# Two of four later modulation sections summed in the output-merge stage, and the residual-gate rows spread by a transpose and a repeating DRAM load

## The chip, the cores and the metric

One core of one Trainium2 chip runs the whole program. The time is device microseconds of one execution. The engines named below are TensorE (PE, with its weight loads as PEld), VectorE (DVE), ScalarE (ACT), GpSimd (POOL) and SyncE (SP). SP, ACT and POOL also issue the transfers between DRAM and on-chip memory; each of them issues its own in program order, among its other work.

## The reference, cut to what matters

The program is one layer of a streaming encoder on 1024 tokens of width 1024, all in float32.

```
mod = silu(c) @ ada_w + ada_b                       # 6 sections of 1024 numbers each
sh1, sc1, g1, sh2, sc2, g2 = split(mod, 6)
h = rmsnorm(x, ln1_g) * (1 + sc1) + sh1
q, k, v, cb, cc, cx, ga, gb = split(h @ w_in)
y_a = stick_breaking_attention(rmsnorm(q), rmsnorm(k), v)
y_b = cb * causal_dwconv3(cc * cx)
merged = sigmoid(ga) * (y_a @ w_branch_a) + sigmoid(gb) * (y_b @ w_branch_b)
x = x + g1 * (merged @ w_out)
h = rmsnorm(x, ln2_g) * (1 + sc2) + sh2
x = x + g2 * ((silu(h @ w_ffn_gate) * (h @ w_ffn_up)) @ w_ffn_down)
```

What matters here is `mod`. Sections 0 and 1 (sh1, sc1) are needed at once and are summed at the start. Sections 2 to 5 are the "later" ones: 2 is g1, the residual gate of the output projection; 3 and 4 are sh2 and sc2, which enter the second normalisation; 5 is g2, the residual gate of the last product. g1 and g2 multiply along the width, which lies in the columns of the tiles there, so they have to stand as a row that is the same on all 128 partitions.

## The kernel before, in words

A float32 product is made of three matmuls: each factor is split into a rounded high part (a copy on ACT, `whi`, `hi`) and a low rest (a subtraction on DVE, `wlo`, `lo`), and high times high, high times low and low times high are added in PSUM. So each weight tile costs ACT one pass and DVE one pass, and each finished PSUM bank costs a pass on DVE or ACT. PE is kept busy by all of this arriving in time; the 128x512 matmul is the unit nearly everywhere.

The stages in order, with their place in the profiled execution: the start (sections 0 and 1 of `mod`, v and k) to about 200 us; q, the convolution and the gates ("gate stage", to about 597 us); attention with the B branch's products as filler (to about 993 us); the product with `w_branch_a` and the merge ("merge stage", to about 1086 us); the output projection and second normalisation; the SwiGLU products; the down projection.

**Gate stage.** The loop over `gates` runs 20 products, each cut Strassen-like into seven block products `p1..p7`; the last eight are the sigmoid gates (sections named 4 and 3 there, four each). The sums of weight blocks (`ws`) are made on POOL, their splits on ACT and DVE, and the results `c` are combined on DVE straight from PSUM (`tt(nc.vector, c.., p.., c.., ...)`, all on line L136). Between them the loop pulls the generator `mods_later`, five steps after each gate of the last eight (`next(ml, None)`).

**mods_later.** For a section, `ada_w` is seen as 8 tiles of 128 x 1024 (`ada_2[q, k]`, 512 KB each): the 128 partitions are 128 outputs, the 1024 columns the inputs. `silu(c)` stands in `cab` on all partitions. One DVE instruction per tile (`tensor_tensor_reduce`, shown on the profile as CUSTOM_DVE_ANT_0 on L640, followed by a short read of its accumulator) multiplies and adds along the columns, and leaves 128 outputs as one column of `msum`. I call it a "section sum". Four sections make 32 of them. The tiles are loaded on ACT's queue into buffers that the gate stage has anyway (`uu`, `sq`, `tr`). For sections 3 and 4 the 8 columns plus bias go to `mod`. For 2 and 5 the columns are spread to a row on all partitions by 8 matmuls each against the identity `dm` (the loop body that line L653 stands for; the profile counts 32 of 128x128 for the two sections, as a float32 matmul is recorded more than once), copied by ACT to `uu`, and written as 512 KB to `d_g[e]` in DRAM. They are loaded back as 512 KB where they are used: `g1b` on ACT's queue at the head of the output projection, `g2b` on SP's queue in the down projection.

**Merge stage.** Sixteen products (m, n) of 24 matmuls each into PSUM banks of the tag `pj`, of which there are two. After each, DVE multiplies the bank by the gate (`sgi`, L1148), adds the stored B branch (`mb`, L1149), ACT takes the high part (L1153) and DVE the rest (L1154). A bank can be written again when its L1148 is done. The weights of the next stage (`w_o`) are loaded and split ahead here by `preload_wo`, at the product (6, 0) in program order. POOL has no work in this stage.

**What sets the order.** The instruction order on each engine is fixed at build time by a list scheduler that works from its own estimates; the engines then run their lists strictly in order. A wait at the head of an engine's list so holds up all that is behind it. Buffers are taken in turn, and a stage's buffers reuse the memory of the stage before it, so a load into a new buffer waits for the last reader or writer of what lay there.

Of the kernel before, what the change touches and what calls it, by code (L numbers as in the profile page):

```python
# [17 lines left out]
P = 128  # L18
T = 1024
D = 1024  # L20
# [10 lines left out]
def block_kernel(tc, x, x_t, cols, ada_1, ada_2, ada_row, w_q, w_kv, w_cg, w_a, w_b, w_o, w_g, w_u, w_d, out):  # L31
# [43 lines left out]
    d_y = drp.tile([KT, P, T], F32, name="d_y")  # L75
    d_mb = drp.tile([KT, P, T], F32, name="d_mb")
    d_b = drp.tile([1, 512], F32, name="d_b")
    d_g = [drp.tile([P, D], F32, name=f"d_g{e}") for e in range(2)]
    d_x1 = drp.tile([KT, P, D], F32, name="d_x1")

    d_t = {q: drp.tile([P, 2, 4, 512], F32, name=f"d_t{q}") for q in (6, 3, 5, 4)}
# [540 lines left out]
    def g_big():  # L622
        return gp.tile([P, T + 2], F32, tag="uu", bufs=2, name=nm("uu"))

    def mods_later():

        csb, cab = g_big()[:, :D], gp.tile([P, D], F32, tag="tr", bufs=2, name=nm("cab"))
        nad = 0
        nc.scalar.dma_start(cab, ada_row[0:1, :].broadcast_to([P, D]))
        nc.scalar.activation(csb, cab, AF.Sigmoid)  # L630
        tt(nc.vector, cab, cab, csb, ALU.mult)
        yield
        for q, sec in enumerate(SECS):
            ms = gp.tile([P, 8], F32, tag="msum", bufs=2, name=nm("msum"))
            for k in range(KT):
                tag = ("uu", "sq", "uu", "sq", "tr")[nad % 5]
                ad = g_big()[:, :D] if tag == "uu" else gp.tile([P, D], F32, tag=tag, bufs=2, name=nm("ad"))
                nad += 1
                nc.scalar.dma_start(ad, ada_2[q, k])
                nc.vector.tensor_tensor_reduce(out=ad, in0=ad, in1=cab, scale=1.0, scalar=0.0, op0=ALU.mult,  # L640
                                               op1=ALU.add, accum_out=ms[:, k:k + 1])
                yield
            if sec in (3, 4):
                tt(nc.vector, mod[:, sec - 1], ms, acol[:, sec - 1], ALU.add)
                continue
            e = 0 if sec == 2 else 1
            tt(nc.vector, ms, ms, gcol[:, e], ALU.add)
            yield
            gb_ = g_big()[:, :D]
            for n in range(2):  # L650
                ps = g_ss()
                for i in range(4):
                    nc.tensor.matmul(ps[:, i * P:(i + 1) * P], ms[:, 4 * n + i:4 * n + i + 1].broadcast_to([P, P]), ident,  # L653
                                     start=True, stop=True)
                nc.scalar.activation(gb_[:, n * 512:(n + 1) * 512], ps, AF.Copy)
            nc.scalar.dma_start(d_g[e], gb_)
            yield

    def g_ss():
        return ps_tr()  # L660
# [69 lines left out]
    for g, (sec, j) in enumerate(gates):  # L730
        raw, raw2 = raws
        p1, p2 = pre[g] if g in pre else (g_prod(g_split(raw[:, :512]), 0), g_prod(g_split(raw[:, 512:]), 1))
        a11, a12, a21, a22 = raw[:, :512], raw[:, 512:], raw2[:, :512], raw2[:, 512:]
        s1, s2_, s3, s4 = (gp2.tile([P, 512], F32, tag=f"ws{q}", bufs=1, name=nm("ws")) for q in range(4))
        with tc.high_priority() if g == 0 else ExitStack():
            tt(nc.gpsimd, s3, a11, a21, ALU.subtract)
            tt(nc.gpsimd, s2_, a22, s3, ALU.subtract)
            w6 = g_split(s2_)
        tt(nc.gpsimd, s1, a21, a22, ALU.add)
        ws4 = nc.gpsimd.tensor_tensor(out=s4, in0=a12, in1=s2_, op=ALU.subtract)  # L740
# [48 lines left out]
        tt(nc.vector, c21, p4, c21, ALU.add)  # L789
        later()  # L790
        put(c21, j + 4, 0)
        if g + 1 == len(gates):
            for _ in eq:
                pass
        for _ in range((5 if sec in (3, 4) else 0) if g + 1 < len(gates) else 50):
            next(ml, None)
    sg2.close()
    sg_.close()
# [300 lines left out]
    fqpool.close()  # L1099


    swx = ExitStack()
    wx = swx.enter_context(tc.tile_pool(name="wpx", bufs=1, side="right", reuse_waits="tile"))
    w_pre = []

    def preload_wo():

        for j in range(3):
            raw = wx.tile([P, 1024], F32, tag="raw", bufs=1, name=nm("raw"))
            nk = 1 if j == 2 else 2  # L1110
# [24 lines left out]
    wa = {}  # L1135
    for m, n in [(0, 0), (1, 0), (0, 1), (1, 1)] + [(m, n) for m in range(2, KT) for n in range(2)]:
        if (m, n) == (KT - 2, 0):
            with tc.issue_after(last_m.ins):
                preload_wo()
        if n == 0:  # L1140
# [11 lines left out]
            mlo[n] = big()  # L1152
        nc.scalar.activation(mh[n][:, m, :], sa, AF.Copy)  # L1153
        nc.vector.tensor_tensor(out=mlo[n][:, m, :], in0=sa, in1=mh[n][:, m, :].bitcast(F32), op=ALU.subtract)  # L1154
    s3.close()
    fpool.close()
    gws.close()
# [27 lines left out]

    los = []
    g1b = dp.tile([P, D], F32, name="g1b")
    nc.scalar.dma_start(g1b, d_g[0])
# [379 lines left out]
    for t in range(4):  # L1568
        nc.scalar.activation(u2t[t], pa[t], AF.Copy)
    with tc.issue_after(last_f[0].ins):  # L1570
        nc.sync.dma_start(g2b, d_g[1])
    pb = [bank() for t in range(4)]
    down(pb, 1, lambda j: R1[j][:, c0])
    for t in range(4):
# [118 lines left out]
```

## Time and profile before

| what | value |
|---|---|
| runs, median (lowest to highest) | 1822.8 us (1822.58 to 1824.99), 3 runs |
| profiled execution, first to last instruction | 1822.9 us |
| granted TensorE clock, mean | 0.995 |
| PE busy / PEld busy | 1794.7 us (98%) / 1492.0 us (82%) |
| DVE / ACT / POOL busy | 1362.9 us (75%) / 809.6 us (44%) / 367.4 us (20%) |
| moved by DMA | 359.57 MB, mean 197 GB/s |
| section sums of `mods_later` (L640) | 32, from 444.1 to 541.2 us |
| spreading matmuls (L653) | 32, in two groups, at 493.9 and 594.9 us |

A matmul row of the trace starts about every 0.227 us in a full run of 128x512 matmuls, though each is shown as 0.39 us long, since they overlap. What PE loses is therefore read from the distance between starts, not from its busy time. The bracket at the end of a timeline row gives idle time in front of the instruction and what ended it.

### The profile page before, as it was taken

Reading aid. Unit: us, or ns where it says so; the run is one execution under the profiler, and the core shown is the slowest. Engines: PE = TensorE matmul, PEld = TensorE weight load, DVE = VectorE, ACT = ScalarE, POOL = GpSimd, SP = SyncE. Lnnn points to the kernel's source line nnn. Section 1 sums busy time; section 2 is a strip of 40 time slices with the busy share of each in tenths; the row PEclk is TensorE's granted clock in tenths of the full one; section 3 lists DMA queues with packets and bytes.
Section 4 is the critical chain, followed back from the end, with each engine's and each line's share of the span. In section 5 each row is a group of like instructions: output and inputs, shape, how many; then the busy total and the mean of one; then the engine's idle time right before and its main releaser. Section 6 shows DMA issues by size and latency. Waiting matters only on the chain.

```text
span 1822.9 us, 24550 instructions
## 1 busy us (share of the span) xinstructions
PE 1794.7 (98%) x8629; PEld 1492.0 (82%) x8629; DVE 1362.9 (75%) x1980; ACT 809.6 (44%) x1510; POOL 367.4 (20%) x277
## 2 busy tenths in 40 slices
PE   8999999999999899999999999999999999999999
PEld 6888877888778788888888888877888888878887
DVE  5876586778894699999997554699877878644776
ACT  5534363333433466666675221764444344322321
POOL 0024234632232000000000000115434444200000
PEclk9999999999999999999999999999999999999999
DMA  9479644223684977696654546424443444299876
GB/s 381 162 247 386 235 163 141 81 98 125 230 287 155 265 203 185 191 336 172 160 135 153 184 155 204 129 91 183 164 150 139 150 169 155 107 347 346 274 230 220
DMA packets 165102, 359.57 MB, mean 197 GB/s; under 512 B 15522, under 2 KB 60906, under 8 KB 163828
## 3 DMA queue, kind: packets, MB, share of 16 engines
q1 hardware_dynamic: 128300, 289.65, 48.6%
q10 hardware_dynamic: 35672, 64.68, 9.9%
q0 software_dynamic: 1008, 3.67, 0.5%
q8 instruction: 69, 1.13, 0.3%
q14 instruction: 53, 0.43, 0.1%
HBM read 247.32 MB, written 110.66 MB: 196 GB/s over the span
## 4 chain that ended last, share of the span: by engine, by line
PE 83%; DVE 8%; DMA 5%; issue 2%; ACT 1%; POOL 0%; SPq 0%; ACTq 0%; DVEq 0%; POOLq 0%
PE e L131 7%; PE e L133 7%; PE e L132 7%; PE pj L293 7%; PE pj L131 5%; PE pj L133 5%; PE pj L132 5%; PE pj L995 4%; PE pj L997 4%; PE pj L996 4%; PE e L1521 4%; PE e L1523 4%; PE e L1522 4%; PE tr L919 3%; PE o L935 2%
## 5 line engine op out<-in xcount | busy, mean ns | idle before, releaser
L905 DVE TENSOR_TENSOR_SCAN pt<-pt,mk 128x128 f32<-128x128 f32 (+7 forms) x128 | 172.6, 1348 | 3.2 <-ACT pt L897 3.2
L131 PE MATMUL e<-big,whi 128*128 128x512 f32 x352 | 138.2, 393 | 3.8 <-ACT c L1421 3.8
L132 PE MATMUL e<-big,whi 128*128 128x512 f32 x352 | 137.9, 392 | 0.0
L133 PE MATMUL e<-big,wlo 128*128 128x512 f32 x352 | 137.8, 392 | 0.0
L293 PE MATMUL pj<-whi,big 128*128 128x512 f32 x448 | 133.7, 396 | 3.1 <-ACT big L262 3.1
L136 DVE TENSOR_TENSOR c<-e,c 128x512 f32<-128x512 f32 x138 | 92.9, 687 | 54.8 <-PE e L133 53.8
L131 PE MATMUL pj<-big,whi 128*128 128x512 f32 x320 | 125.3, 392 | 1.6 <-DVE c L136 1.6
L133 PE MATMUL pj<-big,wlo 128*128 128x512 f32 x320 | 124.9, 390 | 0.0
L132 PE MATMUL pj<-big,whi 128*128 128x512 f32 x320 | 124.6, 389 | 0.0
L122 POOL TENSOR_SCALAR rs_m<-ss 128x1 f32<-128x1 f32 x8 | 1.7, 218 | 607.5 <-ACT xn L1324 607.5
L1521 PE MATMUL e<-whi,f 128*128 128x512 f32 (+1 forms) x319 | 121.8, 382 | 0.9 <-ACT whi L1182 0.6
L1522 PE MATMUL e<-wlo,f 128*128 128x512 f32 (+1 forms) x319 | 121.8, 382 | 0.0
L1523 PE MATMUL e<-whi,f 128*128 128x512 f32 (+1 forms) x319 | 121.6, 382 | 0.0
L136 DVE TENSOR_TENSOR c<-pj,c 128x512 f32<-128x512 f32 x140 | 93.1, 682 | 36.0 <-PE pj L133 35.2
L897 ACT ACTIVATE pt<-z,rq 128x512 f32<-128x512 f32 (+1 forms) x192 | 105.1, 576 | 25.4 <-PE z L896 25.0
L995 PE MATMUL pj<-big,whi 128*128 128x512 f32 x256 | 113.9, 445 | 0.0
L136 POOL TENSOR_TENSOR ws<-raw,raw 128x512 f32<-128x512 f32 x40 | 54.1, 1354 | 278.3 <-DMA raw<-w_cg 130.0
L923 DVE TENSOR_TENSOR atl<-tr,ath 128x512 fp32r<-128x512 f32 (+1 forms) x192 | 103.1, 550 | 9.2 <-ACT ath L922 7.2
L922 ACT ACTIVATE ath<-tr 128x512 fp32r<-128x512 f32 (+1 forms) x192 | 93.2, 488 | 33.1 <-PE tr L919 32.2
L132 PE MATMUL e<-rl,whi 128*128 128x512 f32 x264 | 102.8, 390 | 1.5 <-DVE rl L136 1.5
L133 PE MATMUL e<-rh,wlo 128*128 128x512 f32 x264 | 102.7, 389 | 0.0
L131 PE MATMUL e<-rh,whi 128*128 128x512 f32 x264 | 102.7, 389 | 0.0
(269 smaller groups left out, 4863.2 us busy)
## 6 DMA issues: line engine op xcount, KB each, us to landing
f<-d_f SPq DMA_DIRECT2D x77, 512.0 KB, 4.3
d_f<-fs SPq DMA_DIRECT2D x70, 512.0 KB, 3.2
raw<-w_cg SPq DMA_DIRECT2D x40, 512.0 KB, 3.2
raw<-w_u SPq DMA_DIRECT2D x26, 512.0 KB, 3.3
raw<-w_g SPq DMA_DIRECT2D x25, 512.0 KB, 3.6
raw<-w_kv SPq DMA_DIRECT2D x20, 512.0 KB, 4.0
ad<-ada ACTq DMA_DIRECT2D x19, 512.0 KB, 4.5
ld<-ada SPq DMA_DIRECT2D x16, 512.0 KB, 4.3
```

Of the source, the lines that this page charges most:

```text
L131: nc.tensor.matmul(ps, wh[:, k, :], fh[:, k, :], start=(k == 0), stop=False)
L132: nc.tensor.matmul(ps, wh[:, k, :], fl[:, k, :], start=False, stop=False)
L133: nc.tensor.matmul(ps, wl[:, k, :], fh[:, k, :], start=False, stop=(k == 3))
L136: eng.tensor_tensor(out=out, in0=a, in1=b, op=op)
L293: nc.tensor.matmul(ps, a, b, start=(k == 0 and q == 0), stop=(k == KT - 1 and q == 2))
L897: nc.scalar.activation(pt[:, off + s0:off + s0 + m], z[:, :m], AF.Sigmoid, scale=rq[:, 1, i, h:h + 1])
L905: nc.vector.tensor_tensor_scan(out=pt[:, rev], data0=pt[:, rev], data1=mk[:, rev], initial=1.0, op0=ALU.mult, op1=ALU.max)
L923: nc.vector.tensor_tensor(out=tl[:, :nb, c0:c0 + P], in0=src, in1=th[:, :nb, c0:c0 + P].bitcast(F32), op=ALU.subtract)
L995: nc.tensor.matmul(ps, wh, rh_, start=(k == 0), stop=False)
L1521: nc.tensor.matmul(o, sh, w[0][:, c], start=(j == 0), stop=False)
L1522: nc.tensor.matmul(o, sh, w[1][:, c], start=False, stop=False)
L1523: nc.tensor.matmul(o, sl, w[0][:, c], start=False, stop=(j == NJ - 1))
```

## The change

Of the four later sections, 2 and 4 (g1 and sc2) stay in the gate stage, on the same buffers and ACT's queue, with three generator steps per gate in place of five. Sections 3 and 5 (sh2 and g2) are summed by a second generator `mods_last`, pulled one or two steps after each product of the merge stage and drained before (6, 0). It has a pool of its own: `cab3` for silu(c), loaded again from DRAM and turned by one Silu on ACT, three buffers `ad` for the tiles, and `msum`, `mrow`. Its 18 transfers are issued on POOL's queue. The pool lies where attention's score tiles `pt` lay, and the pool of `preload_wo` is now opened after it is closed.

The two gate rows are no longer spread by matmuls. `msum` is 128 wide and cleared by a POOL memset, transposed by one matmul against the identity, its 8 used rows are copied by ACT and written as 4 KB to `d_g[e]`, which is now one row. `g1b` and `g2b` read that row 128 times (`broadcast_to`).

```
-    d_g = [drp.tile([P, D], F32, name=f"d_g{e}") for e in range(2)]
+    d_g = [drp.tile([1, D], F32, name=f"d_g{e}") for e in range(2)]
...
+    def mod_sums(secs, big_, small, cab, queue, bank_):
+
+        nad = 0
+        for sec in secs:
+            q = SECS.index(sec)
+            ms = small([P, P], "msum")
+            if sec in (2, 5):
+                nc.gpsimd.memset(ms, 0.0)
+            for k in range(KT):
+                ad = big_(nad)
+                nad += 1
+                queue.dma_start(ad, ada_2[q, k])
+                nc.vector.tensor_tensor_reduce(out=ad, in0=ad, in1=cab, scale=1.0, scalar=0.0, op0=ALU.mult,
+                                               op1=ALU.add, accum_out=ms[:, k:k + 1])
+                yield
+            if sec in (3, 4):
+                tt(nc.vector, mod[:, sec - 1], ms[:, :KT], acol[:, sec - 1], ALU.add)
+                continue
+            e = 0 if sec == 2 else 1
+            tt(nc.vector, ms[:, :KT], ms[:, :KT], gcol[:, e], ALU.add)
+            yield
+            ps, row = bank_(), small([P, P], "mrow")
+            nc.tensor.transpose(ps[:, :P], ms, ident)
+            nc.scalar.activation(row[:KT], ps[:KT, :P], AF.Copy)
+            queue.dma_start(d_g[e].rearrange("o (k p) -> (o k) p", p=P), row[:KT])
+            yield
...
-            gb_ = g_big()[:, :D]
-            for n in range(2):
-                ps = g_ss()
-                for i in range(4):
-                    nc.tensor.matmul(ps[:, i * P:(i + 1) * P], ms[:, 4 * n + i:4 * n + i + 1].broadcast_to([P, P]), ident,
-                                     start=True, stop=True)
-                nc.scalar.activation(gb_[:, n * 512:(n + 1) * 512], ps, AF.Copy)
-            nc.scalar.dma_start(d_g[e], gb_)
...
+        yield from mod_sums((2, 4), big_, lambda s, t_: g_tile()[:, :P], cab, nc.scalar, g_ss)
...
-        for _ in range((5 if sec in (3, 4) else 0) if g + 1 < len(gates) else 50):
+        for _ in range((3 if sec in (3, 4) else 0) if g + 1 < len(gates) else 50):
             next(ml, None)
...
+    def mods_last():
+
+        cab = mlp.tile([P, D], F32, name="cab3")
+        with tc.issue_after(lastav[0].ins):
+            nc.gpsimd.dma_start(cab, ada_row[0:1, :].broadcast_to([P, D]))
+            nc.scalar.activation(cab, cab, AF.Silu)
+        yield
+        yield from mod_sums((3, 5), lambda i: mlp.tile([P, D], F32, tag="ad", bufs=3, name=nm("ad")),
+                            lambda s, t_: mlp.tile(s, F32, tag=t_, bufs=1, name=nm(t_)), cab, nc.gpsimd,
+                            lambda: pps.tile([P, 512], F32, tag="tr", bufs=NTR, name=nm("tr")))
...
         if (m, n) == (KT - 2, 0):
+            for _ in ml:
+                pass
+            sml.close()
             with tc.issue_after(last_m.ins):
                 preload_wo()
...
+        for _ in range(1 + m % 2):
+            next(ml, None)
...
-    nc.scalar.dma_start(g1b, d_g[0])
+    nc.scalar.dma_start(g1b, d_g[0][0:1, :].broadcast_to([P, D]))
...
-        nc.sync.dma_start(g2b, d_g[1])
+        nc.sync.dma_start(g2b, d_g[1][0:1, :].broadcast_to([P, D]))
```

The lists of the engines after the change, at three places. Line numbers of the change are a few higher than those before it: the section sum is L640 before and L637 in the change, the gate product on DVE L1148 and L1173, the last filler product's L1044 and L1051.

**DVE where the section sums begin (about 450 us).** Here `c_...<-pj_...` combines a finished PSUM bank, `wlo` splits a weight, and each section sum is two rows (the sum and its read-out). Before:

```order
L723 SCALAR_TENSOR_TENSOR gt_3818<-uu_2776,cst,gt_3818 128x512
L136 TENSOR_TENSOR c_3874<-pj_3878,c_3873 128x512
L136 TENSOR_TENSOR wlo_4010<-raw_3869,whi_4009 128x512
L640 ISA uu_3980,msum_3979<-uu_3980,cab_3975 128x1024
L640 ISA msum_3979 128x1
L136 TENSOR_TENSOR wlo_4033<-ws_4027,whi_4032 128x512
L640 ISA ad_4149,msum_3979<-ad_4149,cab_3975 128x1024
L640 ISA msum_3979 128x1
L136 TENSOR_TENSOR wlo_4083<-ws_4028,whi_4082 128x512
L136 TENSOR_TENSOR c_3873<-pj_3844,c_3873 128x512
```

In the change:

```order
L730 SCALAR_TENSOR_TENSOR gt_3818<-uu_2776,cst,gt_3818 128x512
L136 TENSOR_TENSOR c_3874<-pj_3878,c_3873 128x512
L136 TENSOR_TENSOR wlo_4005<-raw_3869,whi_4004 128x512
L136 TENSOR_TENSOR c_3873<-pj_3844,c_3873 128x512
L637 ISA ad_3984,gt_3979<-ad_3984,cab_3975 128x1024
L637 ISA gt_3979 128x1
L637 ISA ad_4141,gt_3979<-ad_4141,cab_3975 128x1024
L637 ISA gt_3979 128x1
```

Before, three section sums stand ahead of the first of these rows and two more among them, so `c_3873`, which empties the bank `pj_3844`, comes behind five; in the change it comes ahead of all of them.

**DVE where they end before (about 540 us).** Before:

```order
L136 TENSOR_TENSOR wlo_4741<-ws_4702,whi_4740 128x512
L640 ISA uu_4996,msum_4826<-uu_4996,cab_3975 128x1024
L640 ISA msum_4826 128x1
L136 TENSOR_TENSOR wlo_4709<-ws_4703,whi_4708 128x512
L136 TENSOR_TENSOR c_4554<-pj_4617,c_4554 128x512
```

In the change:

```order
L136 TENSOR_TENSOR wlo_4701<-ws_4662,whi_4700 128x512
L1217 SCALAR_TENSOR_TENSOR a_10721<-mod,cst 128x8
L136 TENSOR_TENSOR wlo_4669<-ws_4663,whi_4668 128x512
L136 TENSOR_TENSOR wlo_4719<-ws_4664,whi_4718 128x512
L136 TENSOR_TENSOR c_4520<-pj_4583,c_4520 128x512
```

Before, the last section sum stands between the two `wlo` splits that the next block products need (`wlo_4741` and `wlo_4709`); in the change none stands between `wlo_4701` and `wlo_4669`, which answer to them, and six rows lie between the stage's last sum and `wlo_4701`.

**DVE at the head of the merge stage (about 999 us).** `oy` is attention's last output, `mb_...<-pj_...` the emptying of the last filler product's bank, `ya` splits attention's output, `sgi_...<-pj_...` empties the first merge product. Before:

```order
L941 TENSOR_TENSOR oy_9966<-o_9948,otmp_9965 64x256
L136 TENSOR_TENSOR wlo_10122<-raw_10119,whi_10121 128x512
L136 TENSOR_TENSOR ya_10061<-yr_10059,ya_10061 128x512
L136 TENSOR_TENSOR ya_10066<-yr_10064,ya_10066 128x512
L1044 TENSOR_TENSOR mb_9986<-pj_9938,sgi_9936 128x512
L136 TENSOR_TENSOR wlo_10126<-raw_10119,whi_10125 128x512
L136 TENSOR_TENSOR ya_10071<-yr_10069,ya_10071 128x512
L1148 TENSOR_TENSOR sgi_10084<-pj_10088,sgi_10084 128x512
```

In the change:

```order
L637 ISA ad_10092,msum_10091<-ad_10092,cab_10045 128x1024
L637 ISA msum_10091 128x1
L136 TENSOR_TENSOR wlo_10051<-raw_10048,whi_10050 128x512
L637 ISA ad_10095,msum_10091<-ad_10095,cab_10045 128x1024
L637 ISA msum_10091 128x1
L1051 TENSOR_TENSOR mb_9912<-pj_9864,sgi_9862 128x512
L136 TENSOR_TENSOR wlo_10055<-raw_10048,whi_10054 128x512
L637 ISA ad_10133,msum_10091<-ad_10133,cab_10045 128x1024
L637 ISA msum_10091 128x1
L136 TENSOR_TENSOR ya_9987<-yr_9985,ya_9987 128x512
L136 TENSOR_TENSOR ya_9992<-yr_9990,ya_9992 128x512
L1173 TENSOR_TENSOR sgi_10010<-pj_10014,sgi_10010 128x512
```

Two section sums now stand ahead of the emptying of the last filler bank and a third ahead of the first merge product's; the two `ya` splits have moved behind them. The other thirteen follow among the next seven products' rows: the sixteenth stands in front of the emptying of the eighth product's bank.

More of the change, by code (lines that the diff above doesn't have):

```diff
@@ L623, in g_big @@
         return gp.tile([P, T + 2], F32, tag="uu", bufs=2, name=nm("uu"))
+    def mod_sums(secs, big_, small, cab, queue, bank_):
[23 more added lines that the diff above has]
+            yield
     def mods_later():
         csb, cab = g_big()[:, :D], gp.tile([P, D], F32, tag="tr", bufs=2, name=nm("cab"))
-        nad = 0
         nc.scalar.dma_start(cab, ada_row[0:1, :].broadcast_to([P, D]))
@@ L632, in mods_later, with big_ @@
         yield
[L633 to L648, printed above, removed]
-            gb_ = g_big()[:, :D]
-            for n in range(2):
-                ps = g_ss()
-                for i in range(4):
-                    nc.tensor.matmul(ps[:, i * P:(i + 1) * P], ms[:, 4 * n + i:4 * n + i + 1].broadcast_to([P, P]), ident,
-                                     start=True, stop=True)
-                nc.scalar.activation(gb_[:, n * 512:(n + 1) * 512], ps, AF.Copy)
-            nc.scalar.dma_start(d_g[e], gb_)
-            yield
+        def big_(i):
+            tag = ("uu", "sq", "uu", "sq", "tr")[i % 5]
+            return g_big()[:, :D] if tag == "uu" else gp.tile([P, D], F32, tag=tag, bufs=2, name=nm("ad"))
+        yield from mod_sums((2, 4), big_, lambda s, t_: g_tile()[:, :P], cab, nc.scalar, g_ss)
     def g_ss():
@@ L1099, in block_kernel @@
     fqpool.close()
+    sml = ExitStack()
+    mlp = sml.enter_context(tc.tile_pool(name="mlp", bufs=1, side="right", reuse_waits="tile"))
+    def mods_last():
[7 more added lines that the diff above has]
+                            lambda: pps.tile([P, 512], F32, tag="tr", bufs=NTR, name=nm("tr")))
+    ml = mods_last()
     swx = ExitStack()
-    wx = swx.enter_context(tc.tile_pool(name="wpx", bufs=1, side="right", reuse_waits="tile"))
     w_pre = []
     def preload_wo():
+        wx = swx.enter_context(tc.tile_pool(name="wpx", bufs=1, side="right", reuse_waits="tile"))
         for j in range(3):
```

## The prediction

> **What bounds the kernel now.** I read the busy times first, then who PE waited for, then the stretches in which those waits lie, then the distances between matmul starts there.
>
> ```profile
> PE 1794.7 (98%) x8629; PEld 1492.0 (82%) x8629; DVE 1362.9 (75%) x1980; ACT 809.6 (44%) x1510; POOL 367.4 (20%) x277
> ...
> PE e L131 <- ACT c L1421: 3.8, 1, 3.8
> ...
> PE pj L133 <- DVE wlo L136: 2.0, 1, 2.0
> ...
> PE pj L131 <- DVE c L136: 1.6, 3, 0.7
> ...
> PE z L895 <- DMA skh<-d_k: 1.3, 1, 1.3
> ...
> PE pj L995 <- DVE mb L1044: 1.2, 1, 1.2
> ...
> PE z L896 <- DMA skl<-d_k: 0.8, 1, 0.8
> ```
>
> PE sets the end: all its waits (us in total, times, longest) are a few microseconds of 1823. So two things can gain: matmuls that go away, and these few waits. Those on `wlo` and `c` lie in the gate stage, those on `skh` and `skl` at the head of attention, that on `mb` at the head of the merge stage, that on `c` L1421 in the SwiGLU stage. The stretches (us; busy time and instructions of PE, PEld, DVE, ACT, POOL; granted clock; DMA share; GB/s):
>
> ```profile
> 440.00:480.00 40.00, 38.41 (x167) 30.86 (x166) 39.17 (x55) 13.31 (x23) 14.98 (x8) 1.00 0.74 268
> 505.00:541.00 36.00, 34.97 (x154) 28.45 (x152) 35.19 (x54) 11.80 (x20) 11.32 (x7) 1.00 0.81 279
> 1004.00:1042.00 38.00, 37.96 (x167) 31.45 (x168) 19.76 (x30) 9.47 (x15) 0.00 (x0) 1.00 0.57 189
> ```
>
> In the two stretches where the gate stage makes its section sums DVE is full (39.2 of 40, 35.2 of 36 us), and PE's three and one waits come there. In the first half of the merge stage DVE is free nearly half the time and POOL wholly.
>
> **The change part by part.** The profiled span is 1822.9 us against a median of 1822.8, so the sum is made on 1822.9 with nothing around it.
>
> *Matmuls.* The spreading groups go.
>
> ```profile
> L653 PE MATMUL tr<-dm,msum x32: 271/275/275, 493.9 to 596.6; 128*128 128x128 f32 x32
> ...
> 493.92 1.95 PE L653 MATMUL tr<-dm,msum 128*128 128x128 f32 x16
> ...
> 495.62 0.48 PE L131 MATMUL pj<-big,whi 128*128 128x512 f32 x1
> ```
>
> A group holds PE for 495.62 - 493.92 = 1.70 us, two 3.4 us. Two transposes come in; in the group one record is 1.70/16 = 0.11 us, two records each and the slower hand-over around them make some 0.15 us apiece. Net -3.1 us; both lie on PE's chain.
>
> *Waits of the gate stage.* Sixteen sums leave it.
>
> ```profile
> 455.87 0.39 PE L133 MATMUL pj<-big,wlo 128*128 128x512 f32 x1
> ...
> 456.96 0.47 PE L131 MATMUL pj<-big,whi 128*128 128x512 f32 x1 [0.71 <-DVE c L136]
> ...
> 520.50 1.22 DVE L640 CUSTOM_DVE_ANT_0 ad<-ad,cab 128x1024 f32<-128x1024 f32 x1
> ...
> 538.59 1.62 POOL L740 TENSOR_TENSOR ws<-raw,ws 128x512 f32<-128x512 f32 x1
> ...
> 538.98 2.31 DVE L640 CUSTOM_DVE_ANT_0 uu<-uu,cab 128x1024 f32<-128x1024 f32 x1
> ...
> 541.96 0.50 PE L133 MATMUL pj<-ft,wlo 128*128 128x512 f32 x1 [1.99 <-DVE wlo L136]
> ...
> 530.00:540.00 10.00, 9.97 (x44) 7.78 (x42) 9.23 (x15) 2.72 (x5) 6.21 (x4) 1.00 0.56 196
> 540.00:550.00 10.00, 8.04 (x28) 6.48 (x29) 6.97 (x12) 4.15 (x8) 2.33 (x3) 0.83 0.57 184
> ```
>
> The first wait costs a start-to-start of 1.09 in place of the 0.227 us of an undisturbed run, 0.86 for an idle time of 0.71, so the three together 1.6 + 3 x 0.15 = 2.1 us. They wait for `c`, which in the new list stands ahead of the sums. The fourth is dearer than its 1.99 us: in its ten microseconds PE starts 28 matmuls where the row before has 44, 16 x 0.227 = 3.6 us, and the clock column falls to 0.83. It waits for a `wlo` behind a sum that took 2.31 us beside a POOL instruction, where one without such company takes 1.22. In the new list no sum stands there, and DVE has 16 x 1.15 = 18 us less to do in a stage that it had filled. I take both as gone, -5.7 us; the bounds are 0 (other rows behind POOL's take their place) and -5.7, as the rows hold no more. ACT is relieved of sixteen transfers too, but nothing behind it was PE's last wait.
>
> The fourth wait is a price list for later: idle of 1.99 us brings about 1.6 us of slow clock after it, idle of 1.2 (below) none. [...]
>
> *Head of attention.*
>
> ```profile
> 607.96 0.40 PE L997 MATMUL pj<-big,wlo 128*128 128x512 f32 x1
> ...
> 609.63 0.30 PE L895 MATMUL z<-skh,sqt 128*128 128x128 f32 x1 [1.27 <-DMA skh<-d_k]
> ...
> 610.68 0.30 PE L896 MATMUL z<-skl,sqt 128*128 128x128 f32 x1 [0.75 <-DMA skl<-d_k]
> ...
> d_g<-uu ACTq DMA_DIRECT2D x1, 512.0 KB, 5.6
> ...
> 600.00:610.00 10.00, 8.66 (x44) 6.57 (x42) 1.59 (x3) 0.85 (x2) 0.00 (x0) 1.00 1.14 266
> ```
>
> The loads are late here, about 2.2 us of waiting and some 2 us of slow clock behind it. PE now comes 1.7 us sooner (the second group is gone), and the 512 KB write of the gate row no longer goes through the same full DMA: at 266 GB/s 2.0 us. I take 0. Bounds: +1.7 (the loads come no sooner, so the group's gain is lost here) and -4.2 (waits and slow clock vanish).
>
> *Head of the merge stage.*
>
> ```profile
> 998.75 0.43 DVE L941 TENSOR_TENSOR oy<-o,otmp 64x256 f32<-64x256 f32 x1
> ...
> 1003.20 0.69 DVE L1044 TENSOR_TENSOR mb<-pj,sgi 128x512 f32<-128x512 f32 x1
> ...
> 1004.04 0.47 PE L995 MATMUL pj<-ya,whi 128*128 128x512 f32 x1 [1.17 <-DVE mb L1044]
> ```
>
> PE could have gone on at 1002.7; the wait costs 1.3 us. In the new list two sums and a `wlo` stand between `oy` and `mb`: 999.1 + 1.15 + 0.6 + 1.15 = 1002.0, and `mb` ends near 1002.7, if both tiles have landed. The table load and Silu on ACT take the place of two `w_o` splits. I take -0.7; bounds -1.3 and +2 (the second tile, whose buffer attention's last transposes free at about 990, lands three microseconds late).
>
> *The sums of the merge stage.* A merge product lasts 24 x 0.227 = 5.44 us on PE.
>
> ```profile
> L1148 DVE TENSOR_TENSOR sgi<-pj,sgi x16: 684/692/692, 1007.3 to 1086.0; 128x512 f32<-128x512 f32 x16
> ...
> L639 ACTq DMA_DIRECT2D ad<-ada x19: 334/335/954, 288.2 to 521.8; - x19
> DMA to landing us min/median/max: 3.2/4.5/6.0
> ...
> L1447 POOL DMA_DIRECT2D d_f<-fs x7: 533/533/767, 1597.0 to 1624.1; - x7
> DMA to landing us min/median/max: 7.5/8.0/9.4
> ...
> 500.00:510.00 10.00, 10.00 (x45) 8.27 (x45) 9.32 (x12) 2.52 (x5) 8.02 (x4) 1.00 1.02 391
> ```
>
> DVE's own 19.8 us of the 38 and thirteen sums of 1.22 make 35.6: it fits, with nothing to spare. What decides is whether each tile is there when DVE's list comes to it, since behind a sum that waits stand the `sgi` rows that free the two banks. With three buffers the load of sum k+3 starts when sum k ends. I walked the new list by these durations (0.60 per short row, 1.15 per sum, banks freed by L1173) for several landing times. Up to 6.5 us PE waits for nothing; at 7.0 it loses 0.4, at 7.5 2.4 (waits of 0.9 and 1.5), at 8 4.4, at 9 8.5 us in three waits of 2.4 to 3.0. The price of a landing: 4.5 us on ACT's queue, at most 6.0 in the full gate stage; the only transfers that POOL issues in this trace, writes of the same size, took 7.5 to 9.4. The stage moves 189 GB/s already, and sixteen tiles of 0.52 MB in 40 us add 210; together 399, as much as the fullest row (391). Between 6.0 and 8.0 I take 7.5, nearer to POOL's rows, as queue and load are like theirs: +2.4 us, bounds 0 and +14.2 (9 us, each of its three waits with 1.9 of slow clock).
>
> *Hidden.* The row that `g1b` and `g2b` read 128 times: the like load of `cab` landed in 4.8 us, and there are 17 and 38 us from issue to first use.
>
> ```profile
> L178 ACTq DMA_DIRECT2D cab<-ada_row x1: 418/418/418, 0.7 to 0.7; - x1
> ...
> L1311 DVE TENSOR_TENSOR tm<-e,g1b x16: 681/692/693, 1099.3 to 1179.8; 128x512 f32<-128x512 f32 x16
> ...
> L1188 ACTq DMA_DIRECT2D g1b<-d_g x1: 326/326/326, 1082.0 to 1082.0; - x1
> ```
>
> Without that cover it would be under 5 us. The `w_o` tiles are loaded later, behind the new pool, but the rows still finish before the next stage asks for them. POOL's queue has nothing else in the stage.
>
> Sum: -3.1 - 5.7 + 0 - 0.7 + 2.4 = -7.1; 1822.9 - 7.1 = **1815.8 us**.
>
> **The rivals.**
>
> *A: POOL's tiles come too late.* Place: the sums in the merge stage, behind which the bank-freeing rows stand. At a landing of 9 us the sum is -3.1 - 5.7 - 0 + 14.2 = +5.4: 1828.3 us, slower. It decides from about 8.5 us on (three waits, two with slow clock: 6.5 + 3.8 = 10.3, +1.5). For it: POOL's own rows of 7.5 to 9.4 and the full DMA; against it: those were writes amid three other streams. [...] No row here shows a POOL transfer held up by VectorE.
>
> *B: the gate stage's waits stay.* They come from POOL and DVE getting into each other's way (2.31 against 1.22), and with fewer sums other DVE rows meet POOL. Then -3.1 - 0.7 + 2.4 = -1.4: 1821.5 us, no change. Against it: DVE was full there, and the rows that PE waited for stood behind sums.
>
> *C: more goes than was added.* Tiles land within 6.5 us, the loads of attention's head are in time: -3.1 - 5.7 - 4.2 - 1.3 = -14.3: 1808.6 us. The 3.8 us wait in SwiGLU, in code that the change only shifts, could also go and would give as much.
>
> **How the numbers follow.** Forecast 0.57, A 0.14, B 0.16, C 0.13. A measurement of this kernel tells about 0.2% (3.6 us) from no change. Faster: forecast and C, 0.70; within: B and the mild end of A, 0.19; slower: the rest of A, 0.11. The range leaves out the far halves of A and C: 1807 to 1825 us.
>
> **What would show it.** Right: in the gate stage no PE wait on `c` or `wlo`, no clock below 1.00 there, DVE under 90%; no L653, a single transpose per gate row; in the merge stage sums that wait less than a microsecond for their tile and PE starts every 0.227 us but for one or two gaps of about 1 us. Wrong: POOL's `ad` landing beyond 8 us with PE waiting on `sgi` L1173 and the clock falling (A); a wait on `wlo` or `c` left at 440 to 550 us (B).

## The result, and the profile after

Fourteen executions of each: before 1824.18 us (median), the change 1820.20 us, ratio 0.9978 with a 95% interval of 0.9969 to 0.9987, that is -4.0 us (-5.7 to -2.4). The forecast was -7.1 us. The profiled execution of the change has a span of 1817.7 us and took 1819.48 us; the span before was 1822.9, so the two traces differ by 5.2 us. The 1.8 us between a span and its time are the same in the change and in every experiment; the prediction put nothing there, and its 1815.8 is the span that it forecast rather than the time.

The busy times and PE's waits in the profile of the change (us in total, times, longest):

```profile
PE 1790.8 (99%) x8599; PEld 1487.9 (82%) x8599; DVE 1361.0 (75%) x1980; ACT 807.6 (44%) x1509; POOL 369.5 (20%) x297
...
PE pj L1002 <- DVE mb L1051: 3.2, 1, 3.2
PE pj L293 <- ACT big L262: 2.6, 1, 2.6
PE e L131 <- DVE c L136: 2.5, 1, 2.5
...
PE z L902 <- issue: 1.7, 1, 1.7
PE z L903 <- DMA skl<-d_k: 1.1, 1, 1.1
```

The waits on `wlo` and `c` of the gate stage (L131 and L133 into `pj`) are gone. The wait for `mb` at the merge stage's head has gone from 1.2 to 3.2 us, and is now the longest single one. For the first score's wait (L902, 1.7 us) the view names nothing that ended it ("issue"). Stretches of the change, columns as before:

```profile
440.00:480.00 40.00, 40.00 (x178) 33.14 (x177) 34.28 (x49) 15.92 (x27) 11.91 (x9) 1.00 0.73 254
505.00:541.00 36.00, 36.00 (x161) 29.78 (x160) 29.12 (x45) 13.84 (x25) 12.37 (x8) 1.00 0.42 142
540.00:550.00 10.00, 10.00 (x46) 8.27 (x45) 6.08 (x10) 4.77 (x8) 0.91 (x1) 1.00 0.42 131
...
1004.00:1042.00 38.00, 38.00 (x168) 31.20 (x167) 32.23 (x56) 9.17 (x16) 4.96 (x10) 1.00 0.85 305
996.00:1002.00 6.00, 4.02 (x11) 3.19 (x12) 5.85 (x10) 0.63 (x1) 1.24 (x3) 0.72 0.89 266
```

In the gate stage PE is busy without a break at full clock (46 matmuls from 540 to 550 us, where there were 28), and DVE has fallen to 34.3 of 40 and 29.1 of 36 us. The 38 us of the merge stage that hold the moved sums are unbroken too, with DVE at 32.2. The loss is in the last row: six microseconds with eleven matmuls and a clock of 0.72. "Slow clock" below means such a stretch behind a wait, in which 128x512 matmuls start about 0.43 us apart in place of 0.227.

Where the time went is read from the same places in both traces: PE's last attention score (`z`), its last attention output (`o`), and the last matmul of the merge stage. Before:

```profile
976.86 0.39 PE L896 MATMUL z<-skl,sqt 128*128 128x512 f32 x1
...
995.71 0.28 PE L935 MATMUL o<-atl,vt 128*128 128x128 f32 x1
...
1085.54 0.39 PE L997 MATMUL pj<-ya,wlo 128*128 128x512 f32 x1
```

After:

```profile
967.49 0.39 PE L903 MATMUL z<-skl,sqt 128*128 128x512 f32 x1
...
987.62 0.28 PE L942 MATMUL o<-atl,vt 128*128 128x128 f32 x1
...
1081.42 0.39 PE L1004 MATMUL pj<-ya,wlo 128*128 128x512 f32 x1
```

From score to output 18.85 us became 20.13, and from there to the end of the merge stage 89.83 became 93.80. The change comes to its last score 9.4 us early and leaves the merge stage 4.1 us early. The same differences between PE's matmul starts for every run (us; "gate" from 303 us to the last gate product, "head" on to the first score, "scores" to the last one):

| kernel | gate | head | scores | to last output | merge stage | last two | rest |
|---|---|---|---|---|---|---|---|
| before | 291.64 | 14.92 | 367.23 | 18.85 | 89.83 | 108.68 | 733.03 |
| the change | 283.25 | 13.55 | 367.46 | 20.13 | 93.80 | 113.93 | 732.39 |
| no Silu | 283.82 | 13.49 | 367.16 | 20.31 | 92.44 | 112.75 | 731.95 |
| late sums | 284.48 | 13.52 | 368.64 | 20.26 | 90.21 | 110.47 | 731.41 |
| both | 284.16 | 13.76 | 367.09 | 20.04 | 89.64 | 109.68 | 732.70 |
| both, again | 283.82 | 13.54 | 367.22 | 20.23 | 89.63 | 109.86 | 732.59 |
| no last sections | 284.16 | 13.66 | 369.13 | 18.84 | 88.94 | 107.78 | 735.04 |
| spreading alone | 288.08 | 13.37 | 366.22 | 18.84 | 91.17 | 110.01 | 732.39 |
| move alone | 287.39 | 14.07 | 366.02 | 23.04 | 91.56 | 114.60 | 730.87 |
| two buffers | 283.82 | 13.29 | 367.08 | 20.57 | 92.21 | 112.78 | 732.97 |
| late loads | 283.49 | 13.51 | 367.13 | 18.84 | 93.17 | 112.01 | 733.54 |
| loads after | 283.48 | 13.77 | 368.09 | 18.85 | 97.31 | 116.16 | 733.37 |

The head of the merge stage in the change, ACT, DVE and PE (start, us, engine, line, operation; the bracket is idle time and what ended it):

```profile
989.52 0.63 ACT L1153 ACTIVATE ya<-yr 128x512 fp32r<-128x512 f32 x1 [3.54 <-DMA yr<-d_ya]
990.17 1.28 ACT L1117 ACT_TABLE_LOAD   x1
991.46 1.06 ACT L1117 ACTIVATE cab<-cab 128x1024 f32<-128x1024 f32 x1
992.43 0.61 ACT L1153 ACTIVATE ya<-yr 128x512 fp32r<-128x512 f32 x1
992.95 0.60 ACT L946 ACTIVATE otmp<-o,vlast 64x128 f32<-64x128 f32 x2
...
993.79 0.43 DVE L948 TENSOR_TENSOR oy<-o,otmp 64x256 f32<-64x256 f32 x1
994.14 1.21 DVE L637 CUSTOM_DVE_ANT_0 ad<-ad,cab 128x1024 f32<-128x1024 f32 x1
...
995.28 0.68 DVE L136 TENSOR_TENSOR wlo<-raw,whi 128x512 fp32r<-128x512 f32 x1
995.89 1.21 DVE L637 CUSTOM_DVE_ANT_0 ad<-ad,cab 128x1024 f32<-128x1024 f32 x1
...
997.14 0.69 DVE L1051 TENSOR_TENSOR mb<-pj,sgi 128x512 f32<-128x512 f32 x1
...
997.98 0.47 PE L1002 MATMUL pj<-ya,whi 128*128 128x512 f32 x1 [3.19 <-DVE mb L1051]
```

Before, the same two ACT rows:

```profile
997.36 0.63 ACT L1131 ACTIVATE ya<-yr 128x512 fp32r<-128x512 f32 x1 [0.28 <-DMA yr<-d_ya]
997.90 0.60 ACT L939 ACTIVATE otmp<-o,vlast 64x128 f32<-64x128 f32 x2
```

From `oy` on, the change does what the prediction wrote: two sums and a `wlo`, 3.35 us, and then `mb`. Both tiles were there. What it had not reckoned with is that `oy` itself is late: the last `ya` ahead of it starts 4.81 us after PE's last output (992.43 - 987.62), before 1.65 us (997.36 - 995.71), so 3.16 us later. Two things stand ahead of it in ACT's list: the `yr` load, which came only at 989.5, and the table load with Silu, 2.3 us. (The table load is not an additional one: the kernel before has one at 1212.7 us, in the SwiGLU stage, where the change has none.)

The sums behind it wait for little, 3.0 us in all in three waits. The loads of the tiles on POOL's queue, those behind 960 us:

```profile
L636 POOL DMA_DIRECT2D ad<-ada x16: 527/527/538, 976.1 to 1032.0; - x16
DMA to landing us min/median/max: 3.5/6.1/7.6
```

6.1 us in the median, not the 7.5 that the prediction chose; up to 6.5 us the prediction's walk of DVE's list has PE wait for none of these sums.

### The profile page after: what moved, and what is told of

Same layout as the page of the kernel before. It is cut to its first block, busy times and chain, and to the rows that moved or that the text cites. A ratio compares the mean times of both kernels' runs of the same rounds, so it can differ in the third digit from the quotient of the medians.

```text
span 1817.7 us, 24506 instructions
## 1 busy us (share of the span) xinstructions
PE 1790.8 (99%) x8599; PEld 1487.9 (82%) x8599; DVE 1361.0 (75%) x1980; ACT 807.6 (44%) x1509; POOL 369.5 (20%) x297
## 4 chain that ended last, share of the span: by engine, by line
PE 82%; DVE 7%; DMA 5%; ACT 3%; issue 2%; POOL 1%; ACTq 0%; SPq 0%; DVEq 0%; POOLq 0%
PE pj L293 9%; PE e L132 7%; PE e L133 7%; PE e L131 7%; PE pj L133 6%; PE pj L131 6%; PE pj L132 6%; PE pj L1002 4%; PE pj L1003 4%; PE pj L1004 4%; PE e L1549 4%; PE e L1548 4%; PE e L1550 4%; PE tr L926 3%; PE o L942 2%; PE z L902 2%
## 5 line engine op out<-in xcount | busy, mean ns | idle before, releaser
L131 PE MATMUL e<-big,whi 128*128 128x512 f32 x352 | 137.9, 392 | 2.9 <-DVE c L136 2.5
L133 PE MATMUL e<-big,wlo 128*128 128x512 f32 x352 | 137.7, 391 | 0.0
L131 PE MATMUL pj<-big,whi 128*128 128x512 f32 x320 | 125.0, 391 | 0.0
L133 PE MATMUL pj<-big,wlo 128*128 128x512 f32 x320 | 124.8, 390 | 0.0
L516 ACT ACTIVATE whi<-raw 128x512 fp32r<-128x512 f32 x108 | 67.1, 627 | 83.1 <-PE pj L132 47.5
L136 DVE TENSOR_TENSOR wlo<-raw,whi 128x512 fp32r<-128x512 f32 x108 | 83.9, 781 | 26.9 <-ACT whi L516 26.8
L133 PE MATMUL e<-rh,wlo 128*128 128x512 f32 x264 | 102.7, 389 | 0.0
```

The costliest lines, as they stand in the source:

```text
L131: nc.tensor.matmul(ps, wh[:, k, :], fh[:, k, :], start=(k == 0), stop=False)
L133: nc.tensor.matmul(ps, wl[:, k, :], fh[:, k, :], start=False, stop=(k == 3))
L136: eng.tensor_tensor(out=out, in0=a, in1=b, op=op)
```

## The experiments

Each was compared with the kernel before on the same chip; ratios are given with their 95% interval. Most of these intervals overlap that of the change, so what an edit did is read from the stages of its trace.

**No Silu.** The change's silu(c) is written to a row in DRAM in the gate stage and read back.

```
+        nc.scalar.dma_start(d_c, cab[0:1, :])            # in mods_later
...
-            nc.gpsimd.dma_start(cab, ada_row[0:1, :].broadcast_to([P, D]))
-            nc.scalar.activation(cab, cab, AF.Silu)
+            nc.gpsimd.dma_start(cab, d_c[0:1, :].broadcast_to([P, D]))
```

> The change, but silu(c) is kept as a row in DRAM from the gate stage and read back 128 times, so the merge stage's head has no Silu and no table load on ACT. Theory S (those two sit ahead of attention's last outputs on ACT and make `oy`, behind which the two sums and `mb` stand, about 1.8 us late): PE's wait for `mb` falls from 3.2 to about 1.3 us, the slow clock behind it goes, 3.7 us less than the change, span about 1814.0. Rival D (the section tiles fill the DMA, the `yr` loads come late, and ACT would have waited for them anyway): the wait stays at 2.8 us or more, span above 1816.5.

Ratio 0.9969 (0.9957 to 0.9980), span 1816.5. ACT and PE:

```profile
991.32 0.63 ACT L1154 ACTIVATE ya<-yr 128x512 fp32r<-128x512 f32 x1 [0.91 <-DMA yr<-d_ya]
991.86 0.60 ACT L948 ACTIVATE otmp<-o,vlast 64x128 f32<-64x128 f32 x2
...
996.90 0.51 PE L1004 MATMUL pj<-ya,whi 128*128 128x512 f32 x1 [1.91 <-DVE mb L1053]
```

The last `ya` starts 3.50 us after PE's last output (987.82), 1.3 us sooner than in the change, and waits there for its load. So of the 3.16 us Silu and table load are 1.3; the other 1.85 us, by subtraction, are the load's (the run with the loads behind it, below, tries that). Both theories have a part: the wait falls by 1.3 us, not by 1.9, and the slow clock behind it stays. The merge stage is 1.4 us shorter.

**Late sums.** Silu stays; no sum may stand ahead of the emptying of the first merge product on DVE (`first_m[0]`).

```
+                if first_m:
+                    tc.add_manual_dep(s_.ins, first_m[0].ins.name, ...)
```

> The change with its Silu, but no section sum may stand ahead of the emptying of the first merge product's bank on DVE. If the wait for `mb` is `oy` plus two sums plus `wlo`, it falls by 2 x 1.15 to about 0.85 us without slow clock; the later sums then cost about 0.7 us (walk at 6.0 us landing): 3.5 us less than the change, span about 1814.2. If what stands ahead of `oy` sets it alone, the wait stays above 2.5 us and the span above 1816.5.

Ratio 0.9956 (0.9943 to 0.9968), span 1815.5.

```profile
998.15 0.47 PE L1008 MATMUL pj<-ya,whi 128*128 128x512 f32 x1 [1.02 <-DVE mb L1057]
```

The wait fell from 3.19 to 1.02 us, no slow clock follows, and the merge stage is 3.6 us shorter than the change's: taking the two sums from in front of `mb` brings the most of any single edit, with the slow clock that the longer wait brought. The sums and the late `oy` make the loss together: the prediction had room for the sums behind an `oy` that comes in time.

**Both edits**, measured twice.

> Both edits: no Silu and no table load in the merge stage, and no section sum ahead of the first merge product's emptying. Theory S: no wait for `mb` left (0 to 0.3 us), one or two waits of under 1 us on `sgi` behind the sums; 4.4 to 5.2 us less than the change, span about 1813. Rival D: `oy` still late, wait for `mb` 0.5 us or more, span above 1814.

> The kernel with both edits again, beside the one above: 0.9949 to the kernel before, within 0.9937 to 0.9962; 20.0 us from the last score to the last output and 89.6 us from there to the end of the merge stage, within 0.5 us.

Ratios 0.9949 (0.9937 to 0.9962) and 0.9967 (0.9956 to 0.9979), spans 1814.8 and 1814.6. No wait for `mb` is left, and the last two columns of the table are 109.7 and 109.9 us, 4.1 to 4.3 under the change. Some 20.1 us to the last output, in place of 18.85, remain. By its traces this is the fastest kernel of the study that does the whole work; by its times it can't be told from the one with late sums (0.9956), and the second interval overlaps that of the change (0.9969 to 0.9987). The trace has the gain both times at the same place. The second ratio misses the interval expected for it.

**No last sections.** Sections 3 and 5 are left out: no tile is loaded, none summed (zeros instead), no silu(c).

> The change without sections 3 and 5: their tiles are not loaded and not summed (zeros in place of the sums), no Silu; the transpose and the row stay. It gives what the sums of the merge stage cost in all. Theory S with the late `yr` loads at attention's end (about 1 us): 3.2 + 1.9 of wait and slow clock at the merge head less about 1, and 1 us at attention's end: some 5 us less than the change, span about 1812.7. If the merge stage's sums cost more than their head (rival A in a mild form): span below 1811. If the lost time at attention's end has nothing to do with the tiles' transfers, the 1 us stays: span about 1813.7.

Ratio 0.9941 (0.9929 to 0.9953). Its profiled execution is a long one (1818.5 us where the median is 1814.7), so its span of 1816.7 says nothing; its stages do:

```profile
987.52 0.63 ACT L1151 ACTIVATE ya<-yr 128x512 fp32r<-128x512 f32 x1 [0.63 <-DMA yr<-d_ya]
989.88 0.63 ACT L1151 ACTIVATE ya<-yr 128x512 fp32r<-128x512 f32 x1 [1.73 <-PE pj L1006]
990.41 0.60 ACT L948 ACTIVATE otmp<-o,vlast 64x128 f32<-64x128 f32 x2
```

The last `ya` starts 1.04 us after PE's last output and waits for no load but for PE. To the last output it takes 18.84 us, as before. The last two columns are 107.8 us: the merge stage's sums cost the change 6.15 us in all, of which 1.3 lie at attention's end and 4.9 in the merge stage. Above both edits, which keep every sum, it is 1.9 to 2.1 us: so much is left of their cost once they stand in the right place.

**Late loads.** Both edits, and the loads of silu(c) and of the first three tiles held back by a one-column copy on POOL.

```
+            nc.gpsimd.tensor_copy(cab[:, 0:1], yal[1][1][:, 0:1].bitcast(F32))
...
+            if i < 3:
+                nc.gpsimd.tensor_copy(t_[:, 0:1], yal[1][1][:, 0:1].bitcast(F32))
```

> The kernel with both edits (no Silu, no sum ahead of the first merge product's emptying), and in addition the first three tiles and silu(c) are loaded about 5 us later or more, by a one-column copy on POOL from an attention output split late in the stage, ahead of each load. Theory: the transfers beside attention's end delay the `yr` loads and with them ACT's `ath`; then PE's last attention products come 0.7 to 1.3 us earlier against attention's last scores (18.9 to 19.4 us from the last score to the last output in place of 20.0), and the merge stage stays as it was or loses up to 1 us on late tiles: 0.5 to 1.3 us less than the kernel with both edits. Rival: the delay has nothing to do with these transfers: 20.0 us stay.

Ratio 0.9962 (0.9948 to 0.9976), span 1817.3.

```profile
984.79 0.63 ACT L1167 ACTIVATE ya<-yr 128x512 fp32r<-128x512 f32 x1 [0.38 <-DMA yr<-d_ya]
992.48 0.63 ACT L1167 ACTIVATE ya<-yr 128x512 fp32r<-128x512 f32 x1 [7.06 <-DMA yr<-d_ya]
...
995.77 0.47 PE L1010 MATMUL pj<-ya,whi 128*128 128x512 f32 x1 [2.31 <-DVE mb L1059]
```

18.84 us to the last output: the tiles' transfers do delay attention's end. But the next `yr` load now runs beside four transfers at once, ACT waits 7.06 us for it, `oy` is late and the wait for `mb` is back. The gain was handed on, not kept.

**Loads after.** The same with the loads behind the last `ya` that `oy` needs, sums behind the second product's emptying (`first_m[1]`), and two `ya` splits behind the last filler bank's. These are three edits at once.

> The kernel with both edits; silu(c) and the first three tiles are loaded only behind the last attention output that ACT and DVE must split before `oy` (a one-column copy on POOL of that output ahead of the loads), no sum stands ahead of the emptying of the second merge product, and two `ya` splits stand behind the emptying of the last filler bank. Theory (the tiles' transfers delay the `yr` loads that run beside them): no `yr` load before `oy` has company, so 18.85 us from the last score to the last output (20.04 with both edits) and no wait for `mb`; later `yr` loads have company, which costs PE up to 1 us in the third product. Span 1 to 2 us under that of the kernel with both edits in the same call. Rival: the loss only moves to the next load that PE waits for, and the merge stage is longer by what attention's end gains: same time as with both edits.

Ratio 0.9986 (0.9976 to 0.9997), span 1822.3. Attention's end is 18.85 us, and there is no wait for `mb`: the last `ya` ahead of `oy` starts 1.15 us after PE's last output (987.33), so with the loads gone from beside it its lateness is gone too. But behind the third product DVE waits for a tile, with a bank-freeing row behind it (ACT; POOL's landings in this stage; DVE; PE):

```profile
988.48 0.63 ACT L1167 ACTIVATE ya<-yr 128x512 fp32r<-128x512 f32 x1 [1.65 <-DMA yr<-d_ya]
...
DMA to landing us min/median/max: 3.8/6.1/11.8
...
1010.64 0.69 DVE L1191 TENSOR_TENSOR sgi<-pj,sgi 128x512 f32<-128x512 f32 x1
...
1020.38 1.23 DVE L640 CUSTOM_DVE_ANT_0 ad<-ad,cab 128x1024 f32<-128x1024 f32 x1 [1.78 <-DMA ad<-ada]
...
1021.81 0.69 DVE L1191 TENSOR_TENSOR sgi<-pj,sgi 128x512 f32<-128x512 f32 x1 [0.20 <-DMA sgi<-d_sga]
...
1022.56 0.80 PE L1010 MATMUL pj<-ya,whi 128*128 128x512 f32 x1 [5.24 <-DVE sgi L1191]
```

PE stands for 5.24 us: the bank that it needs is freed at 1021.8, and between that row and the emptying before it (1010.64) DVE's list has four sums with splits among them; the fourth sum's tile is 1.78 us late. Slow clock follows. The rival held, and worse than it said: the merge stage is 7.7 us longer than with both edits. This is the mechanism of the prediction's rival A, at a place where the sums have been pushed together.

**Two buffers** for the tiles, in place of three (`bufs=2`).

> The change with two buffers for the merge stage's tiles, not three: the cost of a tile that is late. Walk of DVE's list by the durations of the profile, landing 6.0 us as in the change (median of its POOL loads): waits of PE of 0.6, 1.1, 1.8 and 1.8 us behind the sums beside that for `mb`, +5.5 us, span about 1823; at 5.5 us landing +2.2, at 6.5 us +9.0. If the sums are not what the bank-freeing rows wait for, nothing changes: span 1817 to 1819.

Ratio 0.9975 (0.9964 to 0.9986), span 1816.9: no different from the change.

```profile
DMA to landing us min/median/max: 3.6/5.3/8.1
...
1020.20 0.50 PE L1002 MATMUL pj<-ya,whi 128*128 128x512 f32 x1 [1.53 <-DVE sgi L1173]
```

PE loses 2.2 us behind the sums (0.50 and 1.68 between starts beyond the usual 0.227). The walk has +2.2 at a landing of 5.5, and the landing was 5.3; the 5.5 us that I expected came from taking over the 6.0 of the change. It did not show in the time: with only two tiles loaded at attention's end, the `ya` ahead of the Silu started at 987.2 (989.5 in the change), and the wait for `mb` was 0.97 us.

**Spreading alone**, with all four sections in the gate stage; and **move alone**, with the spreading by matmuls.

> The kernel before with the new spreading alone (transpose, 4 KB row, repeating reads); all four sections are still summed in the gate stage, five steps per gate. By the prediction's steps: two groups of 1.70 us become two transposes, -3.1 us; the gate stage's waits on `c` and `wlo` (5.7 us with the slow clock) stay within 1.5 us of that, since the same thirty-two sums fill DVE: span about 1819.8. Rival: the waits come from the spreading groups, and go with them: span below 1816.

> The change with the old spreading (two groups of matmuls, 512 KB rows written and read): only the sums of sections 3 and 5 move. The gate stage's waits go (-5.7 to -6.6 us), the merge head costs what it costs in the change (wait for `mb` of 3.2 us and some 1.7 us of slow clock, +4.0 against before), attention's end +1.3: span about 1822 (1820.5 to 1823). The second group of 1.70 us now lies in the merge stage. If the 512 KB write of the row is what makes attention's first loads late, the head of attention is longer than in the change by 1 us or more.

Ratios 0.9988 (0.9976 to 1.0000) and 1.0003 (0.9991 to 1.0016): the spreading alone gives some 2 us, barely told from none, the move alone nothing that can be told. Their waits, of the first kernel at the gate stage and at the merge head, and of the second at attention's end:

```profile
534.50 0.47 PE L131 MATMUL pj<-big,whi 128*128 128x512 f32 x1 [1.96 <-DVE c L136]
...
999.28 0.47 PE L993 MATMUL pj<-ya,whi 128*128 128x512 f32 x1 [2.54 <-DVE mb L1042]
```

```profile
991.91 0.39 PE L943 MATMUL o<-ath,vt 128*128 128x256 f32 x1 [2.35 <-ACT ath L931]
```

With the spreading alone the gate stage is 3.56 us shorter: 1.6 for its group, 2.0 less of waits; some 3.8 us of waits stay (by starts; 1.96, 0.53 and 0.81 us of idle time). That is a little outside what I expected, and the rival, by which all of them go, does not hold. With the move alone it is 4.25 us shorter, with 2.2 us of waits left at 472 to 477 us that the change does not have. So each edit alone takes a part of the gate stage's waits, the move the larger one, and only both together take all. Whether what the spreading alone takes comes from its groups or from the other order that the scheduler finds was not tried. In the move alone the loss at the stages' border is as large as in the change (114.60 us, 1.7 of them the group), but it shows as a wait on `ath`, not on `mb`: by my reading the same late `yr` load (ACT waits for `yr` 19.8 us in all there, 16.8 before), another victim. And the spreading alone, with no tile there at all, has a wait of 2.54 us for `mb` in its trace, behind two `ya` splits in DVE's list: that place is tight in the kernel before too. The row of 512 KB is not what makes attention's first loads late. The move alone can't show that, since there the rows are written at 515 and 1065 us, far from attention's head. The spreading alone shows it: it writes 4 KB at 592.4 us, where the kernel before writes 512 KB at 597.5, and its head is 13.37 us against 14.92, shorter by the group less a transpose and no more.

## Why the prediction was right or wrong

By the table (forecast against measured, us):

| step | forecast | measured |
|---|---|---|
| gate stage: one group, one transpose, waits | -1.7 + 0.15 - 5.7 = -7.25 | -8.39 |
| head of attention, with the other group | -1.7 | -1.37 |
| scores of attention | 0 | +0.23 |
| attention's end | no step | +1.28 |
| merge stage: head, sums, one transpose | -0.7 + 2.4 + 0.15 = +1.85 | +3.97 |
| what follows | 0 | -0.64 |
| sum | -7.1 | -4.92 |

(The 0.3 us to the spans' difference of 5.2 lie, net, ahead of the gate stage and behind the last matmul's start.)

*Matmuls*: right. Both groups are gone; around the one transpose of the gate stage the starts are 0.12 us further apart than without it, where I had 0.15.

*Waits of the gate stage*: right in mechanism and a little small, -6.8 (the -8.39 less group and transpose) against -5.7. All four waits are gone, the clock stays at 1.00, and DVE has room. Rival B does not hold for the change, though the move alone shows that it is not far; and the spreading alone already took 2.0 us, which the prediction gave to the sums wholly. Of the 6.8 us, 1.6 are slow clock behind a wait of 1.99 us; by the count in the last section only about half of such waits bring it, so the many executions (-4.0 us) may hold less of this than the two traces (-5.2 us). That was not tried.

*Head of attention*: 0 was right to 0.3 us. The first scores still wait, 1.7 and 1.1 us, the second by name for `skl`: the first `skh` load is issued at 590.5 in place of 599.8 us, 9.3 us sooner, and the first score comes 9.6 us sooner, so the loads moved with PE.

*Head of the merge stage*: this is the step that failed, -0.7 against about +3.8 (2.0 of wait, 1.7 of slow clock). It failed at its first number. I started from `oy` at its old distance from PE and wrote that the table load and Silu "take the place of two `w_o` splits" on ACT. They do not: they stand between two `ya` passes with `otmp` behind them, 1.3 us by the run without Silu. And I had asked only when the tiles would land, not what their landing does to the `yr` loads that run beside them, 1.85 us by the same run, and 1.3 us more at attention's end, for which the prediction had no term. ACT waits for `yr` 16.8 us in all before, 22.8 in the change and 16.7 without the last sections. The runs with the loads moved show that this price follows the loads: 18.84 and 18.85 us at attention's end, and the last `ya` 1.15 us behind PE's last output in the one that holds them back the longest. The bound of +2 was for a late tile; no tile was late.

*The sums of the merge stage*: the walk was right, the landing that I chose was not. At the measured 6.1 us it gives nothing where I had +2.4. POOL's writes of 7.5 to 9.4 us were the wrong rows to price a POOL load by; ACT's loads of the same tiles (4.5, at most 6.0) were nearer. With DVE busy 32.2 of 38 us the loads issued from POOL landed in 6.1 us in the median and 7.6 at most.

The chance of no more than 0.2% either way was 0.19, and the measured -0.22% lies at that border, for a reason that none of the rivals had: a gain in the gate stage larger than forecast, half of it given back where one stage's loads meet the next one's. It is luck that the sum is off by no more: the head of the merge stage and attention's end came out 4.5 and 1.3 us dearer than forecast, and 2.4 us that the tiles did not cost and 1.1 us more from the gate stage made up for more than half of that.

## What to carry to other kernels

Work that was moved to a stage with idle engines was paid for at that stage's border: its first loads ran beside the loads that the stage before still waited for, and its first instructions stood in in-order lists ahead of that stage's last outputs. So price what a moved step is put ahead of, on every engine that it touches (here one activation on ACT and two sums on DVE), and what its transfers run beside, before asking whether its own data will be in time. Where the work has slack, an explicit edge that holds it behind the border's critical rows is cheap: one on DVE brought 3.5 us here (of the table's last two stages); holding back the transfers as well only moved the loss.

## What the runs showed of the hardware

The prediction took it that an idle time of 2 us brings slow clock and one of 1.2 does not. Over twelve traces waits of about 2 us and a little more went either way (14 of 27 brought it, below). The same wait in the SwiGLU stage, in the change and in the kernel with late sums:

```profile
1211.18 0.50 PE L132 MATMUL e<-rl,whi 128*128 128x512 f32 x1 [2.21 <-DVE rl L136]
...
1206.00:1216.00 10.00, 7.79 (x35) 6.13 (x34) 10.00 (x14) 4.95 (x7) 0.00 (x0) 1.00 0.25 77
```

```profile
1210.23 0.50 PE L132 MATMUL e<-rl,whi 128*128 128x512 f32 x1 [2.48 <-DVE rl L136]
...
1206.00:1216.00 10.00, 7.52 (x26) 5.75 (x25) 10.00 (x15) 5.40 (x8) 0.00 (x0) 0.83 0.33 110
```

35 matmuls start in ten microseconds in the one, 26 in the other, at a clock of 1.00 and 0.83. It does not go by the length of the wait: nine of the twelve traces have this one at 2.48 or 2.49 us, and slow clock follows in four of them and not in five. In the twelve traces, behind 300 us and apart from the head of attention (two waits side by side there), 27 gaps between starts are 1.9 to 2.8 us longer than usual; 14 are followed by five to nine matmuls at up to twice the distance (1.1 to 1.6 us lost), 13 by none. Of those of 0.9 to 1.87 us not one is followed by that, those of 3.35 to 5.4 us all are. What decides it in between, these traces do not show. With several such waits in each execution this may be part of why one kernel's executions are spread over several microseconds (1817.0 to 1824.4 for the change); that was not tried by itself.

What stays open: why the gate stage's waits differ between the move alone and the change, whose sums in that stage are the same; and whether the loads at the border could be given a time at which nothing waits for what runs beside them.
